# Moving the transposes of the combined sums behind the next gate-and-up block and the second-last pair's down products

## The chip, the cores and the metric

The kernel runs on one core of one Trainium2 chip. The metric is the device time of one execution in microseconds (us), lower is better. The engines of the core work side by side, each through its own queue in a fixed order: TensorE (PE, matrix products; PEld its weight loads), VectorE (DVE), ScalarE (ACT), GpSimd (POOL) and SyncE (SP, which issues nearly all DMAs here). An instruction waits for the semaphores of the engines whose results it needs, and everything behind it on its engine waits with it.

## The reference, cut to what matters

A decoder trunk of two layers on 256 tokens with 1024 features, float32. A layer is an attention block, then a SwiGLU feed-forward block (FFN), then a gated per-layer embedding (PLE):

```python
u = _rmsnorm(h, ffn_norm_g[i])
gu = u @ ffn_w_in[i]
h = h + (jax.nn.silu(gu[..., :D_FF]) * gu[..., D_FF:]) @ ffn_w_out[i]
gate = jax.nn.sigmoid(_rmsnorm(h, ple_norm_g[i]) @ ple_w_gate[i])
h = h + gate * (p[i] @ ple_w_up[i])
```

D_FF is 2816, which the kernel cuts into 22 blocks of 128 features (f = 0 to 21).

## The kernel before, in words

The residual stream h lies feature-major in one SBUF tile, `gx` (`hx` in the code): 8 blocks of 128 features by 256 tokens. Every matrix product is done in three float32r products of a high and a low part, `mm3` (L100, L101, L102): high by high, high by low, low by high. A block of weights comes by one 512 KB DMA into `raw`; ScalarE makes its high part `whi` (L188; L164 where it goes in two pieces), VectorE the low part `wlo` (L189, L169). There are 6 buffers of each of the three, so a load waits until VectorE has read the block that stood in its buffer, and a split waits until TensorE has used the weights that stood in the buffers of `whi` and `wlo`. ScalarE and VectorE take these splits in one fixed order with all their other work.

The FFN of a layer, function `ffn`, runs like this:

- `up([f])` makes the gate-and-up products of block f, 48 products of 256 columns into one PSUM bank `gu_f`, and then `gated`: VectorE scales the bank by the norm's row (`gut`, L631), ScalarE takes the silu (L638), VectorE multiplies by the up half (L639), ScalarE rounds the product to its high part `fh` (L322), VectorE makes the low part `fl` (L323). Five steps that go to and fro between two engines.
- While f goes from 2 to 18, each pair of blocks is followed by `down`, the down products of the pair before: the upper 512 output features in the plain way into the banks `fo_1_0` and `fo_1_1`, the lower 512 by a seven-product scheme (`products`) into four banks `fs_0` to `fs_3`.
- When f is 18 (`SEVEN`), the seven products are complete, and `combined` adds the four banks up: ScalarE copies `fs_0` out as `m` (L672), VectorE does five additions (L674 to L679) into an SBUF tile `c`, which is token-major. In VectorE's order these additions stand among weight splits.
- `turned(c)` turns `c` back to feature-major: 8 TensorE transposes (L687) into two banks `fc_0` and `fc_1`, and then `residual` (L349): VectorE adds the two banks to h, one instruction of 128x512 each.
- The last two pairs have plain down products for the lower half too: `last(FT - 4, 0)` is 24 products from blocks 18 and 19 into the banks `fo_0_0` and `fo_0_1`, `last(FT - 2, 0)` is 24 from blocks 20 and 21 into the same two. Between them `filler(pp)` puts the PLE's up products, `ple_up`, into four banks `pu_0` to `pu_3`: in layer 0 first 6 products into `pu_0` and 6 into `pu_1` for the first block of weights, 12 for the second block, then the same for `pu_2` and `pu_3`; in layer 1 bank after bank, 6 products of 512 columns each for the first three and 6 of 256 for the last.

PSUM has 8 banks in one pool. A new tile takes a bank that an earlier tile has done with, and its first product waits for that tile's last reader. Two of the eight stay with `fo_1_0` and `fo_1_1` until the end of the FFN, so at this place the others take turns in six.

`ffn` is called once per layer; its layers are told apart below by the first number in a tile's name where there is one (`gu0_20`, `gu1_20`).

Of the kernel before, what the change touches and what calls it, by code (L numbers as in the profile page):

```python
# [24 lines left out]
SEVEN = FT - 4  # L25
# [56 lines left out]
def trunk(ctx: ExitStack, tc: tile.TileContext, pt, w, cst, gf, out):  # L82
# [7 lines left out]
    def bank(name):  # L90
        return ps.tile([P, 512], F32, tag="bank", name=name)
# [119 lines left out]
    def blocks(entry=False, form=None):  # L211

        if form:
            return half(APART, 0, form)
        hi, lo = half(APART, ENTRY * P if entry else 0)
        hi = [hi[:, k * P:(k + 1) * P] for k in range(KT)]
        return hi, lo if entry else [lo[:, k * P:(k + 1) * P] for k in range(KT)]
# [121 lines left out]
    def feature_unit(bks, wt, off, x, start, stop):  # L339

        hi, lo = wt
        for m in range(4):
            o = bks[m // 2][:, (m % 2) * S:(m % 2 + 1) * S]
            mm3(o, (hi[off + m], lo[off + m]), x, start and m % 2 == 0, stop)

    def residual(hf, bks):
        for b in range(2):
            at = hx[:, 4 * hf + 2 * b:4 * hf + 2 * b + 2].rearrange("p m s -> p (m s)")
            nc.vector.tensor_tensor(at, at, bks[b], op=ALU.add)  # L349
# [240 lines left out]
    def ffn(layer, nm, filler, np_):  # L590
# [3 lines left out]
        def up(fs):  # L594

            bks = {f: bank(f"gu{layer}_{f}") for f in fs}

            def step(f, a, wt, k, start):
                o = bks[f][:, a * S:(a + 1) * S]
                if f == a == k == 0:  # L600
                    for n, (w_, x) in enumerate(((wt[0][k], nm.k(k)[0]), (wt[1][k], nm.k(k)[0]), (wt[0][k], nm.k(k)[1]))):
                        mm(o, w_, x, start=n == 0, stop=False, skip_group_check=True)
                else:
                    mm3(o, (wt[0][k], wt[1][k]), nm.k(k), start, k == KT - 1)

            if fs[0] == 0:
                wts = {f: (blocks(form=_BOTH2 if f == 0 else None), blocks()) for f in fs}
                for k in range(KT):
                    if k == 3:
                        nm.turn(1)  # L610
                        nm.square(1)
                    if k == 6:
                        table(AF.Abs_reciprocal_sqrt, nm.ss[:, 0:1])
                    for f in fs:
                        for a in range(2):
                            step(f, a, wts[f][a], k, k == 0 and a == 0)
                nm.root()
                table(AF.Silu, nm.y)
                return fs, bks
            for a in range(2):  # L620
                wt = blocks(form=_BOTH1 if (fs[0], a) in AGAIN else None)
                for k in range(KT):
                    if (fs[0], a, k) == (2, 0, 4):
                        gated(*early)
                    step(fs[0], a, wt, k, k == 0)
            gated(fs, bks)
# [41 lines left out]
        def combined():  # L668

            m43, m1, m52, m76 = [b.rearrange("p (a s) -> p a s", s=S) for b in seven]  # L670
            m = work.tile([P, 2, S], F32, tag="t2k", bufs=3, name=f"m43_{layer}")
            nc.scalar.activation(m, m43, AF.Copy)  # L672
            c = work.tile([P, 4, S], F32, tag="bias", bufs=1, name=f"c{layer}")
            nc.vector.tensor_tensor(c[:, 2], m[:, 0], m52[:, 1], op=ALU.add)  # L674
            nc.vector.tensor_tensor(c[:, 1], m[:, 1], m52[:, 0], op=ALU.add)
            o = c[:, 0:4:3]
            nc.vector.tensor_tensor(o, m, m52, op=ALU.subtract)
            nc.vector.tensor_tensor(o, o, m1[:, 0:1].to_broadcast([P, 2, S]), op=ALU.add)
            nc.vector.tensor_tensor(o, o, m76, op=ALU.add)  # L679
            return c.rearrange("p (t n) s -> p t (n s)", n=2)  # L680

        def turned(c):

            bks = [bank(f"fc{layer}_{b}") for b in range(2)]
            for m in range(4):
                for t in range(2):
                    nc.tensor.transpose(bks[m // 2][:, (m % 2) * S + t * P:(m % 2) * S + (t + 1) * P],  # L687
                                        c[:, t, m * P:(m + 1) * P], ident)
            residual(0, bks)

        def down(f):
            wt = blocks()
            for i in range(2):
                feature_unit(acc[1], wt, 4 * i, prod[f + i], f + i == 0, False)
            products(f // 2)

        def last(f, hf):

            wt = blocks(form={(FT - 2, 0): _BOTH1, (FT - 2, 1): _BOTH1}.get((f, hf)) if layer else None)
            for i in range(2):  # L700
                feature_unit(acc[hf], wt, 4 * i, prod[f + i], hf == 0 and f + i == SEVEN, f + i == FT - 1)

        early = up([0, 1])
        for f in range(2, FT, 2):
            up([f])
            if f > SEVEN:
                turned(c)
            up([f + 1])
            if layer == 0 and f in (6, 8, 10, 12):
                moba[0](f // 2 - 3)  # L710
            if f == FT - 6:
                pp = filler()
            if f == 2:
                seven.extend(bank(f"fs{layer}_{t}") for t in range(4))
                acc[1] = [bank(f"fo{layer}_1_{t}") for t in range(2)]
            if f < FT - 2:
                down(f - 2)
            if f == SEVEN:
                c = combined()
        acc[0] = [bank(f"fo{layer}_0_{t}") for t in range(2)]  # L720
        last(FT - 4, 0)
        filler(pp)
        last(FT - 2, 0)
        residual(0, acc[0])
# [204 lines left out]
    for layer in range(2):  # L929
        nf = Norm(3 * layer + 1)  # L930
        if layer == 0:
            attention(0, nm, fox_bias, first, nf)
        else:
            attention(1, nm, lambda _: (lambda: moba[2]), [], nf)
        got = []
        np_ = Norm(3 * layer + 2)
        ffn(layer, nf, lambda pp=None: ple_in(layer) if pp is None else got.append(ple_up(layer, pp)), np_)
        nm = Norm(3) if layer == 0 else None
        ple(layer, np_, got[0], nm)
# [104 lines left out]
```

## Time and profile before

| | |
|---|---|
| median of 3 runs | 652.5 us (651.53 to 653.88) |
| profiled execution | 651.93 us, of which the trace's span is 650.0 us |
| TensorE busy, in the span | 634.4 us, 5262 products |
| VectorE busy | 523.2 us |
| ScalarE busy | 405.1 us |
| DMA | 125.20 MB, mean 193 GB/s |

A page of the profile gives for each engine its busy time and its share of the span, then the span in 40 slices of 16.25 us with a digit for each engine's busy share in tenths; the row PEclk is the clock that TensorE was granted, in tenths of full speed. The answers used below are the table of waits (engine and line, what released it, total idle time, times, longest), the timeline (start in us from the span's start, duration, engine, line, operation, output and inputs; in brackets the idle time before and what ended it), and tables by stretch of time (busy time of each engine in it, granted clock, DMA). Names in the timeline have lost their numbers: `gu` is any of the `gu_f`.

### The profile page before, as it was taken

The numbers are of one execution on the slowest core, as the hardware profiler recorded it, in microseconds if no ns is written. First come the engines' busy times: TensorE is split into PE (matmuls) and PEld (weight loads), VectorE is DVE, ScalarE is ACT, GpSimd is POOL, SyncE is SP. The second block draws the span as 40 slices with busy tenths as digits, with TensorE's granted clock in tenths as the row PEclk, the third lists the DMA queues.
The fourth block names the chain that finished last, engine by engine and source line by source line (L and its number), as shares of the span: only waits on it lengthen the run. The fifth ranks groups of instructions, "written<-read, shape, count | busy, mean of one in ns | idle before, by whom it ended". The sixth has DMA issues, their size and how long they took to land.

```text
span 650.0 us, 13322 instructions
## 1 busy us (share of the span) xinstructions
PE 634.4 (98%) x5262; PEld 612.7 (94%) x5262; DVE 523.2 (80%) x988; ACT 405.1 (62%) x737; POOL 16.1 (2%) x33
## 2 busy tenths in 40 slices
PE   9999999999999999799999999999999999997996
PEld 7899999999999999799989999999999999996985
DVE  6987976899887787868997787589988868888665
ACT  7957676756555554638876587568555555564672
POOL 1500000000000000000000000000000000000002
PEclk9999999999999999989999999999999999997999
DMA  9889643367554556765687533435756555676501
GB/s 323 299 265 364 235 159 128 121 195 236 190 184 155 189 195 208 240 188 171 210 276 250 191 132 131 130 98 162 227 186 189 186 188 195 195 243 218 188 2 65
DMA packets 37214, 125.20 MB, mean 193 GB/s; under 512 B 3968, under 2 KB 7072, under 8 KB 37152
## 3 DMA queue, kind: packets, MB, share of 16 engines
q1 hardware_dynamic: 36832, 123.91, 57.9%
q8 instruction: 41, 0.67, 0.4%
q10 hardware_dynamic: 320, 0.44, 0.2%
q14 instruction: 21, 0.17, 0.1%
HBM read 123.25 MB, written 4.24 MB: 196 GB/s over the span
## 4 chain that ended last, share of the span: by engine, by line
PE 70%; DVE 14%; DMA 6%; issue 5%; ACT 4%; POOL 0%; DVEq 0%; POOLq 0%; SPq 0%; ACTq 0%
PE gu L102 7%; PE gu L100 6%; PE gu L101 6%; DMA raw<-w 5%; PE pq L100 5%; PE pq L102 4%; PE pq L101 4%; DVE wlo L189 4%; DVE wlo L323 3%; PE wo L100 2%; ACT whi L188 2%; PE wo L102 2%; PE wo L101 2%; PE fo L102 2%; PE fo L100 2%
## 5 line engine op out<-in xcount | busy, mean ns | idle before, releaser
L189 DVE TENSOR_TENSOR wlo<-raw,whi 128x1024 fp32r<-128x1024 f32 (+1 forms) x166 | 197.6, 1195 | 36.4 <-ACT whi L188 36.0
L188 ACT ACTIVATE whi<-raw 128x1024 fp32r<-128x1024 f32 (+1 forms) x166 | 169.1, 1032 | 65.0 <-issue 19.7
L100 PE MATMUL gu<-g,whi 128*128 128x256 f32 x702 | 196.0, 279 | 0.0
L102 PE MATMUL gu<-g,wlo 128*128 128x256 f32 x702 | 195.5, 279 | 0.0
L101 PE MATMUL gu<-g,whi 128*128 128x256 f32 x702 | 195.5, 278 | 0.0
L100 PEld LDWEIGHTS gu<-g,whi 128*128 128x128 f32 x702 | 133.4, 190 | 0.0
L101 PEld LDWEIGHTS gu<-g,whi 128*128 128x128 f32 x702 | 133.3, 190 | 0.0
L102 PEld LDWEIGHTS gu<-g,wlo 128*128 128x128 f32 x702 | 133.2, 190 | 0.0
L100 PE MATMUL pq<-g,whi 128*128 128x256 f32 x256 | 71.2, 278 | 0.0
L102 PE MATMUL pq<-g,wlo 128*128 128x256 f32 x256 | 70.9, 277 | 0.0
L101 PE MATMUL pq<-g,whi 128*128 128x256 f32 x256 | 70.8, 277 | 0.0
L164 ACT ACTIVATE whi<-raw 128x128 fp32r<-128x128 f32 (+1 forms) x72 | 41.8, 621 | 28.4 <-PE gu L101 7.2
L100 PE MATMUL fo<-fh,whi 128*128 128x256 f32 x208 | 57.6, 277 | 0.0
L102 PE MATMUL fo<-fh,wlo 128*128 128x256 f32 x208 | 57.5, 277 | 0.0
L101 PE MATMUL fo<-fl,whi 128*128 128x256 f32 x208 | 57.5, 276 | 0.0
L169 DVE TENSOR_TENSOR wlo<-raw,whi 128x128 fp32r<-128x128 f32 (+1 forms) x72 | 48.1, 687 | 10.8 <-ACT whi L164 10.7
L100 PEld LDWEIGHTS pq<-g,whi 128*128 128x128 f32 x256 | 48.1, 188 | 1.1 <-issue 0.7
L101 PEld LDWEIGHTS pq<-g,whi 128*128 128x128 f32 x256 | 48.1, 188 | 0.1
L102 PEld LDWEIGHTS pq<-g,wlo 128*128 128x128 f32 x256 | 48.1, 188 | 0.0
L638 ACT ACTIVATE tt<-gut 128x256 f32<-128x256 f32 x36 | 14.9, 413 | 49.3 <-DVE gut L631 49.3
L198 DVE TENSOR_TENSOR sums<-raw 128x512 f32<-128x512 f32 x18 | 12.4, 692 | 36.4 <-DMA raw<-w 36.4
L100 PEld LDWEIGHTS fo<-fh,whi 128*128 128x128 f32 x208 | 39.1, 188 | 0.0
(216 smaller groups left out, 1363.1 us busy)
## 6 DMA issues: line engine op xcount, KB each, us to landing
raw<-w SPq DMA_DIRECT2D x212, 512.0 KB, 4.2
d<-d SPq DMA_DIRECT2D x4, 768.0 KB, 10.5
raw<-w SPq DMA_DIRECT2D x8, 256.0 KB, 4.4
bias<-d SPq DMA_DIRECT2D x4, 512.0 KB, 7.6
bias<-cd SPq DMA_DIRECT2D x2, 768.0 KB, 8.7
gx<-w SPq DMA_DIRECT2D x1, 512.0 KB, 6.7
bias<-cd SPq DMA_DIRECT2D x1, 512.0 KB, 8.4
p<-pt SPq DMA_DIRECT2D x2, 256.0 KB, 4.1
```

Source lines behind the costliest of these rows:

```text
L100: mm(o, ah, bh, start=start, stop=False, skip_group_check=True)
L101: mm(o, ah, bl, start=False, stop=False, skip_group_check=True)
L102: return mm(o, al, bh, start=False, stop=stop, skip_group_check=True).ins
L164: nc.scalar.activation(o, raw[:, c], AF.Copy)
L169: nc.vector.tensor_tensor(t[:, a + b0 * P:a + b1 * P], raw[:, b0 * P:b1 * P], f32(ht[:, a0:a0 + (b1 - b0) * P]), op=ALU.subtract)
L188: nc.scalar.activation(hi[:, c], raw[:, c], AF.Copy)
L189: nc.vector.tensor_tensor(lo[:, c], raw[:, c], f32(hi[:, c]), op=ALU.subtract)
L198: nc.vector.tensor_tensor(more[:, 0:2], raw[:, 1:3], raw[:, 0:1].to_broadcast([P, 2, S]), op=ALU.add)
L323: nc.vector.tensor_tensor(lo, src, f32(hi), op=ALU.subtract)
L638: nc.scalar.activation(sg, t[:, 0], AF.Silu)
```

## The change

`turned(c)` is taken out of the loop, where it stood between the two blocks of the last pair, and is called after `last(FT - 4, 0)`:

```diff
         for f in range(2, FT, 2):
             up([f])
-            if f > SEVEN:
-                turned(c)
             up([f + 1])
...
         acc[0] = [bank(f"fo{layer}_0_{t}") for t in range(2)]
         last(FT - 4, 0)
+        turned(c)
         filler(pp)
         last(FT - 2, 0)
         residual(0, acc[0])
```

The instructions are the same in number and kind on every engine; the loads and ScalarE's work stand in the same order as before. TensorE and VectorE get another order at one place in each layer.

TensorE, layer 0, before: the end of block 20's gate-and-up products, the transposes, the start of block 21's.

```order
L101 MATMUL gu_20_3635<-g_161,whi_3669 128x256
L102 MATMUL gu_20_3635<-g_161,wlo_3670 128x256
L687 MATMUL fc_0_3707<-cs,c_3629 128x128 x4
L687 MATMUL fc_1_3708<-cs,c_3629 128x128 x4
L100 MATMUL gu_21_3719<-g_161,whi_3721 128x256
L101 MATMUL gu_21_3719<-g_161,whi_3721 128x256
L102 MATMUL gu_21_3719<-g_161,wlo_3722 128x256
```

TensorE, layer 0, after: the end of the down products of blocks 18 and 19 (`fo_0_1`), the transposes, the start of the PLE's up products (`pu_0`).

```order
L101 MATMUL fo_0_1_3778<-fl_19_3557,whi_3780 128x256
L102 MATMUL fo_0_1_3778<-fh_19_3556,wlo_3781 128x256
L687 MATMUL fc_0_3809<-cs,c_3629 128x128 x4
L687 MATMUL fc_1_3810<-cs,c_3629 128x128 x4
L100 MATMUL pu_0_3821<-phi_3347,whi_3826 128x256
L101 MATMUL pu_0_3821<-plo_3348,whi_3826 128x256
L102 MATMUL pu_0_3821<-phi_3347,wlo_3827 128x256
```

The 8 transposes have moved behind 48 products into `gu_21` and 24 into `fo_0_0` and `fo_0_1`. Layer 1 has the same move.

VectorE, layer 0, before: from the scaling of block 20's bank to the low part of block 21's product.

```order
L631 TENSOR_TENSOR gut_20_3698<-gu_20_3635,row_1644 128x512
L349 TENSOR_TENSOR gx<-gx,fc_0_3707 128x512
L639 TENSOR_TENSOR sg_20_3700<-sg_20_3700,gut_20_3698 128x256
L349 TENSOR_TENSOR gx<-gx,fc_1_3708 128x512
L323 TENSOR_TENSOR fl_20_3704<-sg_20_3700,fh_20_3703 128x256
L189 TENSOR_TENSOR wlo_3892<-raw_3890,whi_3891 128x1024
L189 TENSOR_TENSOR wlo_3924<-raw_3922,whi_3923 128x1024
L631 TENSOR_TENSOR gut_21_3780<-gu_21_3719,row_1644 128x512
L189 TENSOR_TENSOR wlo_3967<-raw_3965,whi_3966 128x1024
L639 TENSOR_TENSOR sg_21_3782<-sg_21_3782,gut_21_3780 128x256
L323 TENSOR_TENSOR fl_21_3786<-sg_21_3782,fh_21_3785 128x256
```

VectorE, layer 0, after, the same stretch.

```order
L631 TENSOR_TENSOR gut_20_3698<-gu_20_3635,row_1644 128x512
L189 TENSOR_TENSOR wlo_3892<-raw_3890,whi_3891 128x1024
L639 TENSOR_TENSOR sg_20_3700<-sg_20_3700,gut_20_3698 128x256
L323 TENSOR_TENSOR fl_20_3704<-sg_20_3700,fh_20_3703 128x256
L189 TENSOR_TENSOR wlo_3924<-raw_3922,whi_3923 128x1024
L631 TENSOR_TENSOR gut_21_3768<-gu_21_3707,row_1644 128x512
L189 TENSOR_TENSOR wlo_3967<-raw_3965,whi_3966 128x1024
L639 TENSOR_TENSOR sg_21_3770<-sg_21_3770,gut_21_3768 128x256
L323 TENSOR_TENSOR fl_21_3774<-sg_21_3770,fh_21_3773 128x256
L349 TENSOR_TENSOR gx<-gx,fc_0_3809 128x512
L349 TENSOR_TENSOR gx<-gx,fc_1_3810 128x512
```

The two additions L349 have gone from either side of `sg_20` to the end of block 21's steps, and one weight split stands in front of `sg_20` instead of behind `fl_20`.

VectorE, layer 1, after, the same stretch from `sg_20` on (before it stand `gut_20`, the first piece of `wlo_7989` and the low part `u` of a piece of the PLE's weights; `wlo_8078` is a block that goes in two pieces).

```order
L639 TENSOR_TENSOR sg_20_7821<-sg_20_7821,gut_20_7819 128x256
L169 TENSOR_TENSOR wlo_7989<-raw_7987,whi_7988 128x896
L323 TENSOR_TENSOR fl_20_7825<-sg_20_7821,fh_20_7824 128x256
L189 TENSOR_TENSOR wlo_8023<-raw_8021,whi_8022 128x1024
L631 TENSOR_TENSOR gut_21_7889<-gu_21_7828,row_5769 128x512
L169 TENSOR_TENSOR wlo_8078<-raw_8076,whi_8077 128x128
L169 TENSOR_TENSOR wlo_8078<-raw_8076,whi_8077 128x896
L639 TENSOR_TENSOR sg_21_7891<-sg_21_7891,gut_21_7889 128x256
L323 TENSOR_TENSOR fl_21_7895<-sg_21_7891,fh_21_7894 128x256
L349 TENSOR_TENSOR gx<-gx,fc_0_7930 128x512
L349 TENSOR_TENSOR gx<-gx,fc_1_7931 128x512
```

Here too the two additions stood on either side of `sg_20` before, and now stand last.

The banks change hands with the order. Before, `pu_0` to `pu_3` took the banks of `gu_20`, `fc_0`, `fc_1` and `gu_21`, so their first products waited for `gut_20`, for the two additions L349 and for `gut_21`. Now they take those of `gu_20`, `gu_21`, `fc_0` and `fc_1`: `pu_1` waits for `gut_21`, `pu_2` for the first addition, `pu_3` for the second.

## The prediction

> **What bounds the kernel now.** I read the busy times first, then TensorE's own waits.
>
> ```profile
> PE 634.4 (98%) x5262; PEld 612.7 (94%) x5262; DVE 523.2 (80%) x988; ACT 405.1 (62%) x737; POOL 16.1 (2%) x33
> ```
> ```profile
> PE fc L687 <- DVE c L679: 8.6, 2, 4.8
> ```
>
> TensorE is busy for 98% of the span. The second row, from the table of TensorE's waits, says that it stood 8.6 us for one thing, twice: the transposes `fc` wait for the last addition of `combined`. So the kernel is TensorE's stream of products with one hole per layer, at the line that the change moves. Next come the timeline around both holes and the table by stretches, for the clock.
>
> ```profile
> 272.71 0.28 PE L102 MATMUL gu<-g,wlo 128*128 128x256 f32 x1
> 276.75 1.97 PE L687 MATMUL fc<-cs,c 128*128 128x128 f32 x8 [3.76 <-DVE c L679]
> ...
> 288.32 0.28 PE L100 MATMUL pu<-phi,whi 128*128 128x256 f32 x1
> ...
> 293.76 0.28 PE L100 MATMUL fo<-fh,whi 128*128 128x256 f32 x1
> ...
> 589.84 0.28 PE L102 MATMUL gu<-g,wlo 128*128 128x256 f32 x1
> 594.94 1.97 PE L687 MATMUL fc<-cs,c 128*128 128x128 f32 x8 [4.83 <-DVE c L679]
> ...
> 606.14 0.40 PE L100 MATMUL pu<-whi,phi 128*128 128x512 f32 x1
> ...
> 610.96 0.28 PE L100 MATMUL fo<-fh,whi 128*128 128x256 f32 x1
> ```
> ```profile
> core 0: us, PE busy (x) PEld busy (x) DVE busy (x) ACT busy (x) POOL busy (x), PEclk, DMA share, GB/s
> 267.36:272.83 5.47, 5.47 (x50) 5.43 (x48) 4.46 (x8) 3.92 (x6) 0.00 (x0) 1.00 0.69 222
> 272.83:276.75 3.92, 0.16 (x3) 0.01 (x1) 3.92 (x6) 2.13 (x3) 0.00 (x0) 0.79 0.73 228
> 276.75:281.90 5.15, 5.15 (x24) 5.15 (x25) 4.67 (x7) 0.83 (x2) 0.00 (x0) 0.50 0.75 236
> 589.96:594.94 4.98, 0.16 (x2) 0.00 (x1) 4.98 (x9) 3.29 (x5) 0.00 (x0) 0.76 0.70 225
> 594.94:599.40 4.46, 4.46 (x21) 4.46 (x22) 4.46 (x8) 0.83 (x2) 0.00 (x0) 0.50 0.82 252
> 643.70:647.10 3.40, 0.06 (x1) 0.00 (x0) 2.09 (x6) 0.72 (x1) 0.56 (x1) 1.00 0.20 77
> ```
>
> The reader is to see that a hole costs more than its length. TensorE's clock is 1.00 ahead of it, 0.79 in the mean over it and 0.50 for the 5.15 us behind it (4.46 us in layer 1). From the 0.79, the clock fell to half 0.42 of 3.92 us before the hole's end, that is about 2.3 us after the last product; from the 0.76, 2.6 us after it in layer 1; and at the kernel's end it held 1.00 for 3.40 us with no product. Transposes and the first half of `gu_21` ran at half speed.
>
> **The change, step by step.** *What goes.* At full clock a product of 256 columns takes 0.114 us (5.47 us for the 48 of `gu_20`). A transpose takes 0.109, from the chain of work elsewhere:
>
> ```profile
> 63.93 1.97 PE pp L533 x18
> ```
>
> From the end of `gu_20` (272.83) to the start of `pu` (288.32) layer 0 takes 15.49 us. Its work, 48 products of `gu_21`, 24 of `fo_0` and 8 transposes, is 72 x 0.114 + 8 x 0.109 = 9.08 us. So 6.41 us can go, of which 3.92 are the hole. In layer 1, 606.14 - 589.96 = 16.18 us for the same work: 7.10. Together 13.51 us, more than the 8.6 of the waits, because the half clock goes with the holes.
>
> *What covers the earlier start.* `gu_21` now follows `gu_20` at once, and `fo_0` follows `gu_21`. These rows are VectorE's last split for each:
>
> ```profile
> 270.74 1.23 DVE L189 TENSOR_TENSOR wlo<-raw,whi 128x1024 fp32r<-128x1024 f32 x1 [0.53 <-ACT whi L188]
> ...
> 588.93 1.23 DVE L189 TENSOR_TENSOR wlo<-raw,whi 128x1024 fp32r<-128x1024 f32 x1 [0.53 <-ACT whi L188]
> ...
> 591.33 1.22 DVE L189 TENSOR_TENSOR wlo<-raw,whi 128x1024 fp32r<-128x1024 f32 x1
> ```
>
> The second half of `gu_21` is wanted at 272.83 + 24 x 0.114 = 275.57 and is ready at 271.97; in layer 1 at 592.70, ready at 590.16; layer 1's `fo_0` weights at 595.43, ready at 592.55. The transposes are wanted at 281.04 and 598.17; `c` is ready where they start now, at 276.75 and 594.94. Margins 2.5 us and more: I take this at nothing.
>
> *What is late next.* TensorE gets to `pu_0` at 281.91 (layer 1: 599.04). `pu_1` waits for `gut_21`, `pu_2` for the first addition of `fc`, and both stand in VectorE's queue behind steps that go to and fro with ScalarE. Durations and hand-overs of layer 0:
>
> ```profile
> 276.60 1.22 DVE L189 TENSOR_TENSOR wlo<-raw,whi 128x1024 fp32r<-128x1024 f32 x1
> 277.74 0.69 DVE L631 TENSOR_TENSOR gut<-gu,row 128x512 f32<-128x512 f32 x1
> ...
> 278.93 0.42 DVE L639 TENSOR_TENSOR sg<-sg,gut 128x256 f32<-128x256 f32 x1
> 279.27 0.69 DVE L349 TENSOR_TENSOR gx<-gx,fc 128x512 f32<-128x512 f32 x1
> 279.86 0.43 DVE L323 TENSOR_TENSOR fl<-sg,fh 128x256 fp32r<-128x256 f32 x1
> ```
> ```profile
> 271.08 3.88 ACT L188 ACTIVATE whi<-raw 128x1024 fp32r<-128x1024 f32 x4
> 278.46 0.42 ACT L638 ACTIVATE sg<-gut 128x256 f32<-128x256 f32 x1 [3.50 <-DVE gut L631]
> 279.39 0.42 ACT L322 ACTIVATE fh<-sg 128x256 fp32r<-128x256 f32 x1 [0.51 <-DVE sg L639]
> ...
> 285.73 1.06 ACT L188 ACTIVATE whi<-raw 128x1024 fp32r<-128x1024 f32 x1 [1.65 <-PE gu L101]
> ```
>
> A VectorE instruction starts 0.08 us before the one ahead has ended, a hand-over between engines takes 0.05, one to TensorE 0.06. Up to `gut_20` nothing changes. From there, in the new order, ends in us: `gut_20` 278.43, a split 279.57 (its `whi`, the last of the four shown, was done at 274.96), L639 279.91; ScalarE `fh_20` 280.37 and the next `whi` 281.35 (before, it waited for `gu_21` on TensorE until 283.01; that wait is gone); its `wlo` 282.62; `gut_21` 283.23; split 284.37, L639 284.71, `fh_21` 285.17, `fl_21` 285.65, the additions 286.26 and 286.87.
> TensorE: 6 products of `pu_0` to 282.59, then it waits for `gut_21` until 283.29: 0.70. 18 products to 285.34, wait for the first addition until 286.32: 0.98. The second addition comes in time. Layer 0 keeps 6.41 - 1.68 = 4.73 us.
>
> Layer 1 has more in VectorE's queue:
>
> ```profile
> 595.93 0.69 DVE L631 TENSOR_TENSOR gut<-gu,row 128x512 f32<-128x512 f32 x1
> ...
> 599.60 0.69 DVE L323 TENSOR_TENSOR u<-u,u 128x512 fp32r<-128x512 f32 x1
> ...
> 604.23 0.28 DVE L169 TENSOR_TENSOR wlo<-raw,whi 128x128 fp32r<-128x128 f32 x1
> 604.74 1.09 DVE L169 TENSOR_TENSOR wlo<-raw,whi 128x896 fp32r<-128x896 f32 x1 [0.23 <-ACT whi L164]
> ```
> ```profile
> 596.65 0.42 ACT L638 ACTIVATE sg<-gut 128x256 f32<-128x256 f32 x1 [3.40 <-DVE gut L631]
> ```
>
> Ends by the same rules: `gut_20` 596.62, the split's first piece 596.83, `u` 597.44, L639 597.78, second piece 598.79, `fl_20` 599.14, a split 600.52 (its `whi` at 599.25, behind `fh_20`), `gut_21` 601.13, two pieces 602.35, L639 602.69, `fh_21` 603.15, `fl_21` 603.63, additions 604.23 and 604.84. `pu` takes 610.96 - 606.14 = 4.82 us, so a product of 512 columns 0.23. TensorE: `pu_0` to 600.42, waits until 601.19: 0.77; `pu_1` to 602.57, waits until 604.29: 1.72. Layer 1 keeps 7.10 - 2.49 = 4.61.
>
> *Behind that.* `pu` then ends at 289.03, against 293.76 before, and the splits behind it wait for TensorE's use of the buffers and move with it. Loads move as VectorE frees their buffers, the first of them by less:
>
> ```profile
> 281.49 0.33 SPq L155 DMA_DIRECT2D raw<-w  x1
> ```
> ```profile
> 296.62 0.31 ACT L164 ACTIVATE whi<-raw 128x128 fp32r<-128x128 f32 x1 [1.10 <-issue]
> ```
>
> It is issued when the split that now ends at 279.57 is done, 1.9 us sooner, lands at about 283.8 (4.2 us, below), and ScalarE will want it at 296.62 - 4.73 = 291.9. So the loads cost nothing. From there TensorE has no hole in the rest of the trace, so the gain stays.
>
> *The sum.* 4.73 + 4.61 = 9.34 us off the profiled 651.93: 642.59. The median, 652.5, is 0.57 above that execution, so I forecast 643.2. The new waits are bounded by nothing (13.51 gained, 639.0) and by waits that eat the gain (652.5); I take the chain's 4.17 us, since each link has its row in this very stretch.
>
> **Does the clock stay up?** The new waits are 1.72 us at most, under the shortest time, 2.3 us, after which it fell. But in layer 1 two of them, 0.77 and 1.72, lie 1.38 us apart.
>
> The Trainium skill, "TensorE: Matmul & The Clock Gate", section "Why this matters for your kernels", wants no idle gap over about 3 us between bursts of products. The trace differs: 2.3 us was enough once. By the page alone the sum stays 643.2. The same page, section "Part 4: PE-mode transpose", speaks against this change: transposes do not count as busy for the gate, so that 8 of them close in front of the new waits would help the clock to fall. By that rule the second rival below would be the forecast.
>
> Against this, the clock in the stretch right behind the 1.97 us of `pp` transposes shown above:
>
> ```profile
> 65.90:69.40 3.50, 3.50 (x40) 2.55 (x40) 3.50 (x18) 3.13 (x12) 0.00 (x0) 1.00 1.00 355
> ```
>
> It stayed at 1.00, and the moved transposes take 0.88 us. I take no fall.
>
> **The rivals.**
> - *The clock falls behind the new waits.* Before, half clock lasted from 275.1 to 281.9, 6.8 us, and costs half of what TensorE works in it. Now TensorE would work in nearly all of it: up to 3.4 us in a layer, half of that if it falls late or recovers sooner. Likeliest in layer 1 alone: 643.2 + 1.7 = 644.9, at most 646.6; in both layers up to 650.0.
> - *No new waits*, if VectorE and ScalarE got through block 21's steps before TensorE wants the banks: 639.0. Against it: the first addition must come 1.7 us sooner in layer 0 and 2.5 in layer 1, and the links of the chain each wait for the one before.
> - *Slower, or no change: late loads hold the chain.* On ScalarE the splits between `fh_20` and the silu of block 21 wait for their loads; if a load is late, `gut_21`, `fl_21` and both additions move back, and TensorE stands at `pu_1` and `pu_2`.
>
> ```profile
> 590.19 0.33 SPq L155 DMA_DIRECT2D raw<-w  x1
> ```
> ```profile
> raw<-w SPq DMA_DIRECT2D x212, 512.0 KB, 4.2
> ```
>
>   Layer 1's last one is issued at 590.19, lands by its median 4.2 us later at 594.4 and is wanted at 599.3, so it costs nothing up to a landing of 9.1 us. It decides in layer 1 at 13.7 us (9.1 + 4.61), or at 10.3 if the clock falls behind the longer wait too (3.4 us less to lose). At 11 us, 2.6 times the median, a layer loses 1.9 + 3.4 us beyond the new waits, and both together give 643.2 + 10.6 = 653.8. Against it: the 4.9 us to spare, and TensorE never waited for a load.
> - *The change does nothing*, if `c` were still the last to come at the new place: it has 4.3 and 3.2 us of margin, so I count this with the case before.
>
> **How the numbers follow.** The forecast 643.2 gets 0.67 (its own range 641.0 to 645.0: the chain's ends off by a microsecond per layer), the fallen clock 0.14, no new waits 0.08, late loads 0.11, of which half comes out about as before, 0.02 still faster, 0.04 slower. About 0.3% (2 us) is what a measurement can tell from no change: faster 0.67 + 0.14 + 0.08 + 0.02 = 0.91, same 0.05, slower 0.04. The range 640.0 to 646.6 reaches from near the case without waits to a fallen clock in one layer.
>
> **What would show it.** In TensorE's waits the row of `fc` goes, and `pu` waiting for `gut` and for `gx` L349 comes, about 1.7 us in layer 0 and 2.5 in layer 1, longest 1.7. PEclk is 1.00 over both places. Between `gu_20`'s end and `pu` lie 9.1 us in each layer. A PEclk of 0.5 behind `pu` is the second rival; a wait of `gu` or `fo` for `wlo` would break the cover; `fc` still waiting for `c` would break the order's effect.

## The result, and the profile after

The changed kernel takes 642.9 us (median of 6 runs, 641.55 to 648.06) against 652.4 us before: ratio 0.987, 95% interval 0.983 to 0.991. The forecast was 643.2 us. The profiled execution took 641.55 us, 639.6 of it the span. The busy times from its page, and then TensorE's table of waits, whole (what waited, for what, us in total, times, longest):

```profile
PE 630.3 (99%) x5262; PEld 608.3 (95%) x5262; DVE 522.6 (82%) x988; ACT 404.9 (63%) x737; POOL 16.3 (3%) x33
```
```profile
PE pu L100 <- DVE gx L349: 2.1, 2, 1.4
PE cold L133 <- PEq L1035: 0.8, 1, 0.8
PE pu L100 <- DVE gut L631: 0.2, 1, 0.2
```

The row of `fc` is gone. `pu` now waits for the additions of `fc` (L349) and for `gut_21`: 0.66 us in layer 0 and 0.19 and 1.39 in layer 1, 2.2 us in all. The timeline of TensorE in both places, with the start of the transposes, of `pu`, of each wait, and of the next `fo_0` products in layer 0:

```profile
280.98 1.03 PE L687 MATMUL fc<-cs,c 128*128 128x128 f32 x8
281.77 0.36 PE L100 MATMUL pu<-phi,whi 128*128 128x256 f32 x1
...
285.41 0.38 PE L100 MATMUL pu<-phi,whi 128*128 128x256 f32 x1 [0.66 <-DVE gx L349]
...
288.24 0.28 PE L100 MATMUL fo<-fh,whi 128*128 128x256 f32 x1
...
592.63 1.04 PE L687 MATMUL fc<-cs,c 128*128 128x128 f32 x8
...
593.42 0.47 PE L100 MATMUL pu<-whi,phi 128*128 128x512 f32 x1
...
595.25 0.50 PE L100 MATMUL pu<-whi,phi 128*128 128x512 f32 x1 [0.19 <-DVE gut L631]
...
598.29 0.50 PE L100 MATMUL pu<-whi,phi 128*128 128x512 f32 x1 [1.39 <-DVE gx L349]
```

The eight transposes take 1.03 us where they took 1.97; the next product starts 0.79 us after the first of them, since a product starts before the one ahead has ended. The table by stretches (busy time of each engine, granted clock, DMA) from the end of `gu_20` to `pu`, and from there to the next `fo_0` products, layer 0 and then layer 1:

```profile
272.84:281.77 8.93, 8.93 (x82) 8.93 (x81) 7.92 (x11) 4.09 (x6) 0.00 (x0) 1.00 0.82 267
281.77:288.24 6.47, 5.81 (x52) 5.61 (x50) 4.96 (x9) 3.99 (x7) 0.00 (x0) 1.00 0.65 199
...
584.47:593.42 8.95, 8.95 (x82) 8.95 (x81) 8.85 (x15) 4.84 (x9) 0.00 (x0) 1.00 0.77 228
593.42:600.50 7.08, 5.50 (x28) 4.03 (x26) 6.07 (x9) 4.23 (x9) 0.00 (x0) 1.00 0.74 241
```

TensorE is busy through all of the first and third stretch, and the clock is 1.00 in all four, the new waits included. From the start of `gu_20` to those `fo_0` products layer 0 took 26.40 us before and takes 20.89, layer 1 26.47 and 21.50: 5.51 + 4.97 = 10.48 us, which is the whole difference of the spans (650.0 - 639.6 = 10.4).

Counted as the prediction counts, from the end of `gu_20`, the gains are 5.53 and 4.97 us where it summed 4.73 and 4.61. Of the 0.80 and 0.36 us more, 0.15 and 0.13 come from the stretch ahead of `pu` (8.93 and 8.95 us instead of 9.08). The rest comes from the new waits: from `pu` to `fo_0` it takes 6.47 and 7.08 us, 1.03 and 2.26 more than the 5.44 and 4.82 of before, where the prediction had 1.68 and 2.49 more. (The table of waits shows less, 0.66 and 1.58, because it counts idle time only from the end of the last product.)

Two things asked for experiments: that the new waits are shorter than forecast, and that the new kernel's times scatter over 6.5 us.

### The profile page after: what moved, and what is told of

Read it like the earlier page. It is cut to its first block, busy times and chain, and to the rows that moved or that the text cites. A ratio compares the mean times of both kernels' runs of the same rounds, so it can differ in the third digit from the quotient of the medians.

```text
span 639.6 us, 13330 instructions
## 1 busy us (share of the span) xinstructions
PE 630.3 (99%) x5262; PEld 608.3 (95%) x5262; DVE 522.6 (82%) x988; ACT 404.9 (63%) x737; POOL 16.3 (3%) x33
## 4 chain that ended last, share of the span: by engine, by line
PE 91%; DVE 4%; issue 2%; ACT 2%; POOL 0%; POOLq 0%; DVEq 0%; ACTq 0%
PE gu L100 11%; PE gu L102 11%; PE gu L101 11%; PE pq L100 5%; PE pq L101 5%; PE pq L102 5%; PE fo L100 3%; PE fo L102 3%; PE fo L101 3%; PE wo L100 2%; PE wo L102 2%; PE wo L101 2%; PE fs L102 2%; PE fs L100 2%; PE fs L101 2%
## 5 line engine op out<-in xcount | busy, mean ns | idle before, releaser
L100 PEld LDWEIGHTS gu<-g,whi 128*128 128x128 f32 x702 | 131.8, 188 | 0.0
L101 PEld LDWEIGHTS gu<-g,whi 128*128 128x128 f32 x702 | 131.8, 188 | 0.0
L169 DVE TENSOR_TENSOR wlo<-raw,whi 128x128 fp32r<-128x128 f32 (+1 forms) x72 | 48.1, 686 | 10.4 <-ACT whi L164 10.3
L198 DVE TENSOR_TENSOR sums<-raw 128x512 f32<-128x512 f32 x18 | 12.4, 690 | 35.1 <-DMA raw<-w 35.1
L101 PEld LDWEIGHTS fo<-fl,whi 128*128 128x128 f32 x208 | 39.1, 188 | 0.0
```

What stands on the lines that cost most here:

```text
L100: mm(o, ah, bh, start=start, stop=False, skip_group_check=True)
L101: mm(o, ah, bl, start=False, stop=False, skip_group_check=True)
L169: nc.vector.tensor_tensor(t[:, a + b0 * P:a + b1 * P], raw[:, b0 * P:b1 * P], f32(ht[:, a0:a0 + (b1 - b0) * P]), op=ALU.subtract)
L198: nc.vector.tensor_tensor(more[:, 0:2], raw[:, 1:3], raw[:, 0:1].to_broadcast([P, 2, S]), op=ALU.add)
```

## The experiments

**The changed kernel once more, and the move in one layer alone.** The edits of the second and third kernel, the same with the layers exchanged:

```diff
-            if f > SEVEN:
+            if f > SEVEN and layer == 1:
                 turned(c)
...
         last(FT - 4, 0)
+        if layer == 0:
+            turned(c)
```

> The changed kernel once more, to see how far its times scatter (641.55 to 648.06 us in six runs, where the kernel before lay between 651.5 and 653.9). Theory A, the prediction's: the hole and the half clock behind it are gone, only short bank waits at pu are left; then the times lie close together at about 642 to 643, and the scatter was chance. Theory B: the new waits at pu (0.66 us in layer 0, 0.19 and 1.39 in layer 1) let the clock fall in some executions, as the second rival had it; then some runs are again 2 to 6 us longer, with a lower mean clock, and if the profiled run is one of these, PEclk shows 0.5 behind pu in one or both layers.

> The transposes move in layer 0 alone. Theory A: the hole and the half clock behind it count, less the wait at pu. By the trace of after layer 0 took 20.89 us from the start of gu_20 to the last fo_0 product block against 26.40 before: 5.51 off 652.4, 646.9 us. Theory C, that the half clock is hidden and only the idle time counts: 3.76 - 0.66 = 3.1 off, 649.3 us. In both the wait of fc for c stays once, 4.8 us long, in layer 1.

> The transposes move in layer 1 alone. Theory A: by the trace of after layer 1 took 21.50 us from the start of gu_20 to the last fo_0 product block against 26.47 before: 4.97 off 652.4, 647.4 us. Theory C, only the idle time counts: 4.83 - 1.39 - 0.19 = 3.25 off, 649.1 us. If the two layers don't touch one another, the gains of this kernel and of the one that moves in layer 0 alone add up to the whole change's 9.5 us. Theory B: this layer has the longer wait (1.39 us), so the scatter of the whole change should be here and not in the other one.

Measured against 651.9 us before: the changed kernel 641.6 (639.23 to 645.39; ratio 0.986, 0.983 to 0.989); layer 0 alone 647.3 (six runs, 0.993, 0.990 to 0.996; a seventh took 2262 us and is left out); layer 1 alone 649.0 (0.994, 0.992 to 0.996). By the ratios the parts gain 4.5 and 3.8 us, together 8.3 against 9.3 for the whole, whose interval reaches from 7.5 to 11.0: within what these runs can tell they add up. They do not part theory A from C: the interval for layer 0 (2.5 to 6.5 us) holds both.

The times did not lie close together, as theory A has it, but neither is the scatter where theory B puts it: each layer alone scatters over 6.1 us, and so does the old order over 5.5 us in the 23 runs beside them. The scatter is no mark of the new order.

The profiled execution of the repeat was a long one, 645.39 us (span 643.4), and its waits and its clock show that theory B is not the reason there:

```profile
PE pu L100 <- DVE gut L631: 3.4, 2, 1.8
PE pu L100 <- DVE gx L349: 2.0, 2, 1.4
```

The clock stayed at full speed (0.999 in the mean). The waits at `pu` are 5.5 us instead of 2.2 (summed before rounding), since `gut_21` came later. Here are, in the order of time, the step of VectorE in layer 0 that differs most, the last addition of `c`, the additions of `fc`, and the last addition of `c` in layer 1, first from the profile after, then from the repeat:

```profile
248.90 0.69 DVE L198 TENSOR_TENSOR sums<-raw 128x512 f32<-128x512 f32 x1 [2.70 <-DMA raw<-w]
...
275.23 0.68 DVE L679 TENSOR_TENSOR c<-c,fs 128x512 f32<-128x512 f32 x1
...
284.68 1.28 DVE L349 TENSOR_TENSOR gx<-gx,fc 128x512 f32<-128x512 f32 x2
...
588.38 0.68 DVE L679 TENSOR_TENSOR c<-c,fs 128x512 f32<-128x512 f32 x1
```
```profile
251.47 0.69 DVE L198 TENSOR_TENSOR sums<-raw 128x512 f32<-128x512 f32 x1 [3.83 <-DMA raw<-w]
...
277.71 0.68 DVE L679 TENSOR_TENSOR c<-c,fs 128x512 f32<-128x512 f32 x1
...
287.15 1.28 DVE L349 TENSOR_TENSOR gx<-gx,fc 128x512 f32<-128x512 f32 x2
...
592.26 0.68 DVE L679 TENSOR_TENSOR c<-c,fs 128x512 f32<-128x512 f32 x1
```

From `c` to the additions it is 9.45 us in the first and 9.44 in the second: that chain is the same. But all of VectorE runs 2.5 us later, while TensorE gets to `pu` only 0.37 us later (282.14). Following the difference through the FFN of layer 0, from 165 us on, where VectorE is 0.4 us behind, each step of more than 0.15 us by which it falls further behind stands at L198, the first of three additions that `sevenfold` makes from a freshly loaded block: VectorE waits there for the load. In layer 1 the difference goes up and down, by up to 1.4 us a step, mostly at L198 too. The next `fo_0` products of layer 1 start 3.88 us later, which is the difference of the two spans (643.4 - 639.6). The rows of the wait at L198 in the three tables of waits, before, after, and the repeat:

```profile
DVE sums L198 <- DMA raw<-w: 36.4, 12, 4.9
```
```profile
DVE sums L198 <- DMA raw<-w: 35.1, 12, 4.4
```
```profile
DVE sums L198 <- DMA raw<-w: 39.5, 12, 4.5
```

This gives a new theory, D, so far argued from two profiles: VectorE, held up by loads, sets the time of this place; in the old order TensorE waits for it at the transposes, in the new one at `pu`.

A table from five profiles supports it. It is worked out from rows like those above: when `c` is complete, when the next `fo_0` products start, and the time between.

```
                      layer 0                     layer 1
old order
 before               276.69  293.76  17.07       594.88  610.96  16.08
 other layer moved    278.90  296.05  17.15       588.27  603.67  15.40
new order
 after                275.91  288.24  12.33       589.06  600.50  11.44
 after, again         278.39  290.73  12.34       592.94  604.38  11.44
 this layer alone     276.58  288.93  12.35       596.98  608.42  11.44
```

In the new order the time from `c` onward is the same to 0.02 us (one more profile, of the last set below, has 12.42 and 11.43), whatever TensorE did ahead. What varies is when `c` comes: over 3.0 us in layer 0.

**The hole filled with work.** The old order, with products of zeros in the hole (`still` is a constant zero):

```diff
             if f > SEVEN:
+                warm_ = bank(f"warm{layer}")
+                for _ in range(18):
+                    mm(warm_, still.to_broadcast([P, P]), still.to_broadcast([P, 512]), start=True, stop=True)
                 turned(c)
```

> The order of before, with 18 products of zeros (512 columns, 0.23 us each, 4.1 us in all, in a bank of their own that nobody reads) ahead of the transposes in each layer: the transposes still wait for c, but TensorE works meanwhile. Theory A, half clock counts: c comes when it came before, the clock stays 1.00, and the 5.15 us in layer 0 and 4.46 in layer 1 that ran at half clock shrink by half, 2.58 and 2.23, less some 0.3 by which the zeros overshoot in layer 0: 4.4 off, 648.0 us. Theory C, the half clock behind the hole is hidden by something else that ends last: 652.4 us, no change.

Measured: 649.8 us, ratio 0.9971 (0.9958 to 0.9984), 1.9 us less with an interval of 1.0 to 2.7. Both theories miss. In its profile TensorE still waits 0.24 and 1.84 us for `c`, the clock behind that is 1.00, and from `c` to the next `fo_0` products it takes 15.18 and 14.34 us, 1.89 and 1.74 less than before:

```profile
277.07:286.45 9.38, 9.38 (x80) 9.38 (x81) 8.07 (x11) 3.27 (x6) 0.00 (x0) 1.00 0.73 241
...
594.84:604.23 9.39, 9.39 (x81) 9.39 (x82) 8.71 (x14) 3.41 (x7) 0.00 (x0) 1.00 0.77 240
```

So the half clock counts, but less than I reckoned. One reason is that I took it from one execution, whose mean clock of 0.987 is the lowest that the old order shows: 42 runs of it have 0.987 to 0.993, 0.989 in the mean. This kernel has 0.998, so that the loss of clock is usually (0.998 - 0.989) / (0.998 - 0.987), 0.8 of the profile's, and by this estimate 3.6 us become 2.9. What a milder fall is, the profile with layer 0 alone moved shows in layer 1, where the hole was 3.03 us; the stretches are the hole, and two behind it:

```profile
585.20:588.33 3.13, 0.10 (x2) 0.00 (x1) 3.13 (x5) 1.45 (x3) 0.00 (x0) 0.93 0.72 242
588.33:590.50 2.17, 2.17 (x10) 2.17 (x11) 2.17 (x3) 0.42 (x1) 0.00 (x0) 0.50 0.82 221
590.50:593.00 2.50, 2.50 (x21) 2.50 (x20) 2.50 (x7) 0.42 (x1) 0.00 (x0) 0.84 0.81 277
```

From 0.93 and 0.84 the clock was half from 587.9 (2.7 us into the hole) to 591.3: 3.4 us, not the 6.8 of the profile before. The estimate of 2.9 us still lies just outside the interval of 1.0 to 2.7; what makes up the rest is not shown.

**`c` later, and `c` without banks and additions of its own.** The first makes `c` later, and so its margin smaller. The second adds `c`, turned, into the banks of `fo_0`:

```diff
-            nc.vector.tensor_tensor(o, m, m52, op=ALU.subtract)
+            for _ in range(4):
+                nc.vector.tensor_tensor(o, m, m52, op=ALU.subtract)
```
```diff
-            bks = [bank(f"fc{layer}_{b}") for b in range(2)]
...
-                    nc.tensor.transpose(bks[m // 2][...], c[:, t, m * P:(m + 1) * P], ident)
-            residual(0, bks)
+                    mm(acc[0][m // 2][...], c[:, t, m * P:(m + 1) * P], ident, start=False, stop=False, ...)
```

> The changed order with c made late on purpose: the subtraction m - m52 of combined stands four times instead of once (the same result each time), 3 x 0.60 us more on VectorE in each layer; the planned order on VectorE then puts gut_20 and the multiplication behind its silu ahead of the last two additions of c, nothing on TensorE moves. In the trace of after c came 5.1 us (layer 0) and 3.6 us (layer 1) before the transposes wanted it. Theory M, that these margins are margins of the kernel: no change, 642 us. Theory D, that VectorE's queue sets the time here and TensorE's wait at pu for gut_21 and for the additions only hides it: gut_21 and the additions come 1.3 to 1.8 us later in each layer (up to 0.5 may fall into a hand-over), the waits at pu grow by as much, and the time by 2.6 to 3.6 us, to about 645. Theory B, that longer waits at pu let the clock fall: by up to 3.4 us more in a layer, with PEclk 0.5 behind pu.

> The changed order, but c is not transposed into banks of its own: eight products with the unit matrix add it turned into the banks of fo_0, where the down products stand already. The two banks of fc and the two additions behind them on VectorE go; pu_2 and pu_3 then wait only for gut_20 and gut_21. Price: a plain f32 product of 128 columns against a transpose of 0.109 us; between the same 0.109 and 0.23 (four passes of half a 0.114 us product of 256 columns): 0 to 1 us a layer. Theory D: the waits at pu (0.66 and 1.58 us in the one profile, 2.50 and 2.99 in the other) go, because gut_21 is done before pu_3 is reached in both: 641.9 less 2.2 to 5.5, plus 0 to 2: 637 to 641 us, with less scatter. Theory A2, that the additions are not what pu waits for: no change or up to 2 us slower.

The late `c` gave 644.4 us (642.64 to 645.12), 1.5 to 2.8 us above the three sets of the changed kernel (642.9, 641.6 and, below, 642.9). By the times alone this is not shown, since the ranges and the intervals of the ratios overlap (0.984 to 0.990 here; 0.983 to 0.991, 0.983 to 0.989 and 0.981 to 0.987 there). The trace says more. Layer 0, the first addition of `c` and `gut_20`, in the profile after and with the late `c`:

```profile
271.10 0.42 DVE L674 TENSOR_TENSOR c<-m,fs 128x256 f32<-128x256 f32 x1
...
276.96 0.69 DVE L631 TENSOR_TENSOR gut<-gu,row 128x512 f32<-128x512 f32 x1
```
```profile
271.87 0.41 DVE L674 TENSOR_TENSOR c<-m,fs 128x256 f32<-128x256 f32 x1
...
278.33 0.68 DVE L631 TENSOR_TENSOR gut<-gu,row 128x512 f32<-128x512 f32 x1
```

`gut_20` starts 6.46 us after the first addition instead of 5.86, in layer 1 too: two additions of `c` now stand behind it, so it came only 0.60 us later, not 1.3 to 1.8. The next `fo_0` products start 17.74 and 16.95 us after that first addition, against 17.14 and 16.25: 0.60 and 0.70 later, although `c` itself, by the same count, was complete 3.9 us later. That is against theory M, and against the sizes that I gave theory D. It also says that in the new order the place does not hang on `c` itself: `c` marks how late VectorE is, and the chain to `pu` starts at `gut_20` (7.72 us from there to the additions in the profile after, 7.71 with the late `c`, in layer 0). The waits at `pu` came to 3.8 us, and a new one appeared: `fo_0` stood 1.0 us in layer 1 for the last of the four subtractions, whose bank it takes over. The clock was 0.998 with waits of up to 1.4 us, so theory B found nothing here either.

Adding into `fo_0` gave 640.7 us (639.95 to 641.64). The waits at `pu` are gone from its profile, and the products with the unit matrix take 1.70 us where the transposes took 0.79 (16 of them on TensorE, from 280.23 to `pu` at 281.93):

```profile
280.23 1.95 PE L686 MATMUL fo<-cs,c 128*128 128x128 f32 x16
281.93 0.37 PE L100 MATMUL pu<-phi,whi 128*128 128x256 f32 x1
```

The price is 0.91 us a layer, 1.8 in all, the gain the waits of 2.2 to 5.5 us, and the scatter is 1.7 us, where the changed kernel's three sets have 5 to 6.5. VectorE's wait for loads is still there (38.5 us at L198); it no longer reaches TensorE. So what `pu` waited for were the additions and, through the order of the banks, `gut_21`: both waits went at once, and this kernel does not part them. The median is 1.0 to 2.3 us under the three sets; the intervals of the ratios overlap, so the times alone do not show this gain.

**The load wait taken from VectorE.** `sevenfold`'s three additions on GpSimd, in the new and in the old order; the third kernel leaves them on VectorE in the old order, but behind the `gut` of the block just computed:

```diff
-        nc.vector.tensor_tensor(more[:, 0:2], raw[:, 1:3], raw[:, 0:1].to_broadcast([P, 2, S]), op=ALU.add)
-        nc.vector.tensor_tensor(more[:, 2], more[:, 0], raw[:, 2], op=ALU.add)
-        nc.vector.tensor_tensor(more[:, 3], more[:, 2], raw[:, 3], op=ALU.add)
+        nc.gpsimd.tensor_tensor(...)      # the same three
```

> The changed order, with the three additions of sevenfold (L198 to L200, 18 times) on GpSimd instead of VectorE. At L198 VectorE stood 35.1 us in one profile of after and 39.5 in the other for loads, 12 times, and its lag behind the other profile grew there and nowhere else. Theory D, that these load waits set when c, gut_21 and the additions come, and so the time and its scatter: VectorE's wait for loads goes and 18 x 1.3 us of work with it, c comes earlier against gu_20, the waits at pu shrink or go, 638 to 641 us, and less scatter. Rival E: GpSimd's additions are slow (2.13 us for 128x512 elsewhere in the trace, so some 4 us a time against 1.3) and hold the buffers, so loads are issued 1.4 to 2.9 us later and the splits come late in their turn: no gain, or slower, 642 to 650.

> The order of before, with the same three additions of sevenfold on GpSimd. Theory D: c comes earlier against the end of gu_20, so the hole ahead of the transposes (3.76 and 4.83 us) shrinks or goes, the clock with it falls later or not at all, and what the change of order is worth shrinks: 640 to 646 us, under 5 us above the changed order with the same edit, where it is 10 without it. Rival E as there: no gain, or slower. Theory F, that the length of the hole is set by the steps of combined alone (some 5.3 us from L674 to c, which stay): the hole stays near 4 us and the time near 652.

> The order of before, all work on VectorE as there; only the three additions of sevenfold stand a few places later in VectorE's queue, behind gut of the block just computed (some 2.8 us later by the trace of after, where L198 starts at 198.39 and that gut at 201.15). This parts the wait for loads from the work and from GpSimd. Theory D, the wait counts: by then the loads have landed, VectorE's 36 us of waiting at L198 shrink to a few us, c comes earlier, the hole ahead of the transposes shrinks or goes: 640 to 646 us in the old order. Theory G, that it was the 27 us of work taken off VectorE or GpSimd's part that helped: 652 us. Rival E: additions 2.8 us later hold the buffers, loads and splits come late, no gain or slower.

The new order gave 639.6 us (638.75 to 640.27), the old one 640.15 (639.58 to 640.53), against 652.8 before: ratios 0.980 (0.977 to 0.984) and 0.981 (0.979 to 0.984). TensorE's order is the same as without the edit; on VectorE some 10 of the 934 other instructions stand elsewhere. The old order with this edit is faster than the changed kernel. Its profile, TensorE's waits and the transposes in the timeline:

```profile
PE cold L133 <- PEq L1036: 0.8, 1, 0.8
PE fc L687 <- DVE c L679: 0.4, 1, 0.4
PE pr L271 <- DVE sh L262: 0.3, 2, 0.2
PE v L452 <- ACT whi L188: 0.3, 1, 0.3
```
```profile
272.90 1.04 PE L687 MATMUL fc<-cs,c 128*128 128x128 f32 x8
...
585.12 1.09 PE L687 MATMUL fc<-cs,c 128*128 128x128 f32 x8 [0.41 <-DVE c L679]
```

The hole of 8.6 us is 0.4 us, without a change of TensorE's order. `c` is complete at 272.47 and 585.07, right when `gu_20` ends. VectorE is not less busy for it, 526.5 us against 523.2 before: the 27 us of the additions went, and other instructions grew longer (below). What went is its wait for loads at L198, 36.4 us before; its idle time in all fell by less, from 126.8 us to 112.0. This refutes theory F, and rival E for GpSimd.

The additions behind `gut` gave 676.7 us, 24 more than before. This is a clear miss for theory D's number, and rival E's case:

```profile
PE fs L100 <- ACT whi L323: 11.1, 16, 0.8
PE gu L102 <- DVE wlo L169: 2.3, 2, 1.2
```

There is no wait of `fc` for `c` left here either, nor of VectorE for loads at these additions. But the splits of the sums now come too late for the products that use them, and loads are issued late: SyncE's queue stood 163.3 us for the last of the three additions, 18 times. The edit moved more than the three additions, too: in the planned order one or two products of the next `gu` now stand ahead of the last nine `fs` products, 18 times, and VectorE's and ScalarE's orders differ at over a hundred instructions each. So it is no clean test of theory D. It cannot say how much of the gain on GpSimd comes from the wait and how much from the 27 us of work that left VectorE's queue; that stays open.

**Side by side.** The changed kernel and the two kernels with GpSimd's additions once more, on one chip:

> The changed kernel, beside the next two on one chip. Theory D: 641 to 643 us as in the two sets before, with a scatter of some us, since VectorE still waits for loads at L198.

> The changed order with sevenfold's additions on GpSimd once more, beside the changed kernel: 639.6 us and a scatter under 2 us, so 2 to 3 us under the changed kernel. If the earlier figure was chance: 642.

> The order of before with sevenfold's additions on GpSimd once more, beside the same edit in the changed order. Theory D: what the change of order is worth has gone with the hole: 640.1 us, within 0 to 1 us of the changed order with this edit. If the order still counted by itself: 4 us or more above it.

642.9 us (640.63 to 645.85), 639.6 (639.16 to 640.59) and 640.1 (639.15 to 640.52), with 652.95 before. Both figures for GpSimd repeat within 0.1 us. With the additions on GpSimd the change of order is worth 0.5 us, where it was worth 10, and the ranges overlap. The scatter went in both orders: 1.4 us and less here, against 5.2 and 5.8 for the changed kernel and the one before. The new order with GpSimd's additions has the lowest median, 3.3 us below the changed kernel. TensorE waits for nothing at these places there, and `c` is complete over 8 us before it is wanted.

## Why the prediction was right, point by point

- *Holes and half clock go.* Right. Between `gu_20`'s end and `pu` lie 8.93 and 8.95 us, predicted 9.08. As a term it was sized on an execution with more half clock than most. One reading was off: at half clock ran the transposes and 16 of `gu_21`'s 48 products (24 products in the row of 5.15 us, 8 of them transposes), not its first half; no term hangs on it.
- *What covers the earlier start.* Right: no `gu` or `fo` waits for a split, in any profile of the new order.
- *What is late next.* The places were right: `pu_1` at `gut_21`, and the bank of `fc_0`. The chain was right too: by it, `fo_0` would start 12.34 us (289.03 - 276.69) after `c` in layer 0 and 11.47 (606.35 - 594.88) in layer 1; the table has 12.33 to 12.35 and 11.44. The waits as a term were mis-sized for any single execution: counted from `pu` to `fo_0` beyond its work, 1.68 and 2.49 us predicted, 1.03 and 2.26 in the profile, 3.15 and 3.67 in the repeat, 2.51 and 1.82 in the third profile. That the sum, 4.17, lies among 3.29, 6.82 and 4.33, and the median within 0.3 us of the forecast, is in part luck. I took the start of the chain from the profile of before as if it stood fixed against TensorE. It does not; VectorE's lag at L198 decides it in each execution, and the wait is what remains. What is fixed is the new order's time from `c`. Against the profile of before it gives 17.07 - 12.33 = 4.74 and 16.08 - 11.44 = 4.64 us, close to the 4.73 and 4.61 of the prediction; the old order's time is not fixed (15.40 us in another execution of layer 1).
- *The clock.* No profile of the new order shows a fall at these places. Three of its 18 runs have a mean clock of 0.994 or 0.995 where the others have 0.996 to 0.999, and take 645.9 to 648.1 us: so it may fall in some executions, as the second rival had it. None of these was profiled; this stays open. The rule for transposes of the Trainium skill ("TensorE: Matmul & The Clock Gate", "Part 4: PE-mode transpose"), by which that rival would be the forecast, is thus not borne out as the usual case: 0.79 us of transposes and the waits behind them at 1.00.
- *Late loads.* I set them aside because TensorE never waited for a load. VectorE did, 36 us of it in the two FFNs, and something like that rival happened in a small way: at L198, ahead of `c`, not between `fh_20` and the silu where I had put it, and worth some 3 us between two executions (5.5 against 2.2 us of waits), not 10.

The prediction never asked why `c` was late. That was not needed for its number, but it is where the rest of the time lay.

## What to carry to other kernels

A wait that disappears when an order is changed may only have moved: measure from the event that was late (here the last addition of `c`, as a mark of how late VectorE is) instead of from the engine that waited, and see what is fixed. Then follow the late engine's own queue back to where it stood idle. Here the moved transposes hid that VectorE was late, and taking the three additions that waited for loads out of its queue gave more than the move and made the move nearly worthless.

## What the runs showed of the hardware

VectorE slows down beside GpSimd, but not in all its instructions. Three groups of VectorE's instructions (count, then busy time and mean in ns), first of the changed kernel, then with the additions on GpSimd:

```profile
L639 DVE TENSOR_TENSOR tt<-tt,gut 128x256 f32<-128x256 f32 x36 | 15.1, 419 | 0.0
L651 DVE TENSOR_TENSOR dif<-tt 128x256 f32<-128x256 f32 x18 | 7.6, 423 | 0.4
...
L631 DVE TENSOR_TENSOR gut<-gu,row 128x512 f32<-128x512 f32 x44 | 30.0, 685 | 0.4 <-PE gu L102 0.4
```
```profile
L198 POOL TENSOR_TENSOR sums<-raw 128x512 f32<-128x512 f32 x18 | 41.1, 2284 | 456.2 <-DVE g L236 261.0 <-DMA raw<-w 82.4 <-ACT tt L638 44.1
...
L639 DVE TENSOR_TENSOR tt<-tt,gut 128x256 f32<-128x256 f32 x36 | 23.1, 642 | 0.0
L651 DVE TENSOR_TENSOR dif<-tt 128x256 f32<-128x256 f32 x18 | 13.1, 730 | 0.5
...
L631 DVE TENSOR_TENSOR gut<-gu,row 128x512 f32<-128x512 f32 x44 | 29.9, 684 | 2.1 <-PE gu L102 1.9
```

The two that read both operands from SBUF take 642 and 730 ns in the mean instead of 419 and 423; `gut`, which reads one operand from a PSUM bank, is unchanged. GpSimd's own addition takes 2284 ns in the mean against VectorE's 690. The mean hides two cases: of the 36 products `tt`, 23 still take 414 to 421 ns, and 13 take 952 to 1514. Each of the 13 starts while a GpSimd addition runs and ends just behind it, as here:

```profile
217.00 1.61 POOL L199 TENSOR_TENSOR sums<-sums,raw 128x256 f32<-128x256 f32 x1
217.94 0.95 DVE L639 TENSOR_TENSOR tt<-tt,gut 128x256 f32<-128x256 f32 x1
```

The Trainium skill, "SBUF — State Buffer", section "SBUF: two separate sides", has a VectorE instruction with two SBUF inputs and a GpSimd instruction that reads SBUF take turns at one pair of ports, each for a whole instruction; these rows agree. It still paid: in TensorE's waits no row names the longer instructions.
